# Transposing the residual in one visit per part, at other places in TensorE's order

## The chip, the cores and the metric

The kernel runs on one core of one Trainium2 chip. The metric is the device time of one execution in microseconds (us); smaller is better. Three executions of the kernel before took 1199.17, 1199.78 and 1201.17 us; their median, 1199.78 us, is the number that the change is compared with.

## The reference, cut to what matters

One decoder layer for 256 tokens of width 2048, in float32. The two places of the change are the two RMS norms behind a residual sum:

```python
x = x + mix @ w_out[i]                                   # w_out: 2048 x 2048

h2 = rms_norm(x, mlp_norm[i])
x = x + jnp.square(jax.nn.relu(h2 @ w_ffn_up[i])) @ w_ffn_down[i]   # 2048 x 8192, 8192 x 2048

gate = jax.nn.sigmoid(rms_norm(x, ple_norm[i]) @ w_ple_gate[i])
x = x + gate * (p[i] @ w_ple_proj[i])
...
return rms_norm(x, final_norm)
```

## The kernel before, in words

Every float32 operand is split into a high part and a rest (`wh` and `wl` for a weight, `h` and `l` for an activation), and a product is made of three float32r matmuls. A weight is loaded in blocks of 512 KB (`raw`, three buffers, by SyncE's DMA queue); ScalarE (ACT) copies it to `wh` in two halves (L149), VectorE (DVE) subtracts to get `wl` (L150). `wh` and `wl` have three buffers each as well, so the split of a block waits until TensorE (PE) is through with the block three places ahead of it. These splits have a raised priority in the scheduler.

The residual `xr` holds the tokens on the partitions, two tiles `x0` and `x1` of 128 tokens each. A product with `xr` as its input needs it the other way round. `transposed(name)` gives for that a function `part(norm, n)`, n from 0 to 3: it turns 512 columns of the residual, with 8 transposes of 128x128 on PE (L1018) into a pair of PSUM banks (`h2t` or `h3t`, the tag "wide" of the pool `psw`, which has two such pairs), and brings them to SBUF in four chunks of 128 columns, each with one ACT copy that scales by the norm's weight (L1024, the high part) and one DVE operation (L1025, the rest). Both read the same pair of banks, and the chunks of a pair follow each other: an ACT copy waits for the DVE operation of the chunk before it.

The stages around the change are these.

- **w_out**: four products `o0` to `o3` of 512 columns each, 48 matmuls of 512 columns each (four blocks of 12); behind each, `residual` adds it to `xr` on DVE (L956). Part n of `h2` follows `o`n in the code.
- **FFN up**: `gemm_wide` for 16 tiles, in two halves each of four blocks (`u00_0` to `u00_3` are the four blocks of the first half of tile 0). Block kq needs the chunks k = 4kq to 4kq+3 of `h2`, that is part kq. A chunk takes 4 matmuls, two of 512 columns (L997) and two of 256 (L1001).
- **FFN down**: `down_sweep` for two halves of the hidden units and two halves of the columns; the last sweep (names `d11`) writes the columns 1024 to 2047. Its four accumulators in the wide banks are released by DVE adds (L1131) after the step of kp 11, four steps before the last, and its other four banks at its end. `keep` splits blocks of the gate's weight ahead of time (`gk`, from `graw`).
- **p @ w_ple_proj**: four short products `pp0` to `pp3`, one block and 12 matmuls each, with ACT copies of the results out of PSUM (L1230). They use the bank pool `psm`. Three of the four square sums of the gate's norm (`junk`, L258) run there too, on ACT.
- **gate**: products `gt0` to `gt3`, which need all of `h3`.

PE's order up to the end of `w_out`'s first half is written by hand (`tc.manual_schedule` for PE, held open in `order`). From there on the scheduler orders all engines by priority; it may put the transposes anywhere between the matmuls once their inputs are expected to be ready. Parts 0 and 1 of `h3` read the columns 0 to 1023, which an earlier sweep finished; they are called from within the last sweep, by `between`, and parts 2 and 3 right behind it.

Of the kernel before, what the change touches and what calls it, by code (L numbers as in the profile page):

```python
# [40 lines left out]
def trunk(  # L41
# [931 lines left out]
    for g_ in o_a:  # L973
        finish(g_)
    order.close()
    rctx.close()
# [5 lines left out]

    def gemm_wide(src, acts, name, consume):

        for half in range(2):
            bank = wide_bank(f"{name}_w{half}")
            for kq in range(4):
                raw = load_raw(src[half, kq].rearrange("p a n -> p (a n)"), 1024, f"{name}{half}_{kq}")  # L990
                for a, (wh, wl) in enumerate(split_w(raw, f"{name}{half}_{kq}")):
                    for b in range(2):
                        k = kq * 4 + 2 * a + b
                        hl = acts(k)
                        for ct in range(2):
                            c = slice(b * 256 + ct * 128, b * 256 + ct * 128 + 128)
                            nc.tensor.matmul(  # L997
                                bank[:, ct, :].rearrange("p (s t) -> p s t", s=2), wh[:, c], hl,
                                start=k == 0, stop=False, skip_group_check=True,
                            )  # L1000
                            nc.tensor.matmul(  # L1001
                                bank[:, ct, 0:T], wl[:, c], hl[:, 0, :], start=False, stop=k == 15, skip_group_check=True
                            )
            consume(half, bank)

    def transposed(name):
# [3 lines left out]

        def part(norm, n):
            for j2 in range(2 * n, 2 * n + 2):
                if j2 % 2 == 0:
                    b = wide_bank(f"{name}t")
                for jj in range(2):
                    j = 2 * j2 + jj
                    for tt in range(2):
                        nc.tensor.transpose(  # L1018
                            b[:, j2 % 2, jj * T + tt * 128 : jj * T + (tt + 1) * 128], xr[tt][:, j * 128 : (j + 1) * 128], ident
                        )  # L1020
                for jj in range(2):
                    j = 2 * j2 + jj
# [9 lines left out]
    for n in range(4):  # L1032
        run(gemm_toks(w_out[n], mix, f"o{n}", lambda banks: residual(banks, n), (6, 7, 2, 3)))
        h2_part("mlp_norm", n)

# [52 lines left out]

    def down_sweep(hf, pair, ys, sboxes, hooks=(), between=None, seven=SEVEN):

# [42 lines left out]
        for q, kp in enumerate((0, 2, 1, 4, 3, *range(5, 16)) if pair else range(16)):  # L1133
# [32 lines left out]
            if kp == seven[-1]:  # L1166
# [9 lines left out]
                add(1, 1, b5)  # L1176
                if between is not None:
                    between()
        for n, tt, c in (("2", 0, 0), ("4", 1, 0), ("3", 0, 1), ("x", 1, 1)):
# [3 lines left out]
    def ffn_half(hf):  # L1183
        sboxes = {}
        ys = []
        for i in range(8):
# [12 lines left out]

            gemm_wide(w_up[f], h2, f"u{f}", square)  # L1200
            ys.append(y)
# [3 lines left out]
        if hf == 1:  # L1205
            h3_part, h3 = transposed("h3")
            h3_box.append(h3)

        down_sweep(hf, 0, ys, sboxes)
        if hf == 0:  # L1210
            down_sweep(hf, 1, ys, sboxes)
        else:
            down_sweep(hf, 1, ys, sboxes, {5: keep, 8: keep, 11: keep, 14: keep}, lambda: [h3_part("ple_norm", n) for n in range(2)], (1, 3, 6, 11))
            for n in range(2, 4):
                h3_part("ple_norm", n)

    ffn_half(0)
    ffn_half(1)
    h3 = h3_box[0]

# [5 lines left out]
    for n in range(4):  # L1226
# [4 lines left out]

        run(gemm_toks(w_proj[n], lambda k: (ph[:, k * T : (k + 1) * T], pl[:, k * T : (k + 1) * T]), f"pp{n}", copy_out))
    fn = a8(0, "fn")
    nc.sync.dma_start(fn, fnorm.partition_broadcast(128))
# [131 lines left out]
```

## Time and profile before

| | |
|---|---|
| median of three runs (lowest, highest) | 1199.78 us (1199.17, 1201.17) |
| the profiled execution, its own time | 1201.35 us |
| its span, first to last instruction | 1199.6 us |
| PE busy, share of the span | 1179.5 us, 98% |
| DVE busy | 868.5 us, 72% |
| ACT busy | 689.8 us, 58% |
| mean granted TensorE clock | 0.997 |

The durations below come from the profiled execution, which has 1.75 us around its span and took 1.57 us more than the median. In the timelines, the first column is the start in us from the span's beginning and the second the duration of the row's instructions together; "x8" is a row of eight instructions. A matmul's row lasts longer than the distance to the next one, since matmuls overlap: costs on PE are taken as differences of starts.

### The profile page before, as it was taken

The numbers are of one execution on the slowest core, as the hardware profiler recorded it, in microseconds if no ns is written. First come the engines' busy times: TensorE is split into PE (matmuls) and PEld (weight loads), VectorE is DVE, ScalarE is ACT, GpSimd is POOL, SyncE is SP. The second block draws the span as 40 slices with busy tenths as digits, with TensorE's granted clock in tenths as the row PEclk, the third lists the DMA queues.
The fourth block names the chain that finished last, engine by engine and source line by source line (L and its number), as shares of the span: only waits on it lengthen the run. The fifth ranks groups of instructions, "written<-read, shape, count | busy, mean of one in ns | idle before, by whom it ended". The sixth has DMA issues, their size and how long they took to land.

```text
span 1199.6 us, 18428 instructions
## 1 busy us (share of the span) xinstructions
PE 1179.5 (98%) x7060; PEld 1010.6 (84%) x7060; DVE 868.5 (72%) x1149; ACT 689.8 (58%) x1276; POOL 18.1 (2%) x69
## 2 busy tenths in 40 slices
PE   8999999999999999999999999999999999999997
PEld 6999988987887888888888788888888888777886
DVE  7687987965656666666878888666667879787552
ACT  6857566566545565555655564454555555668544
POOL 4000010000000000000000000000000000000000
PEclk9999999999999999999999999999999999999999
DMA  6463542354445555555665656655555556766531
GB/s 246 154 201 109 175 144 104 113 198 141 140 163 179 184 185 190 192 191 189 201 201 200 193 195 211 191 181 188 189 184 189 207 194 197 287 231 211 195 120 70
DMA packets 60328, 216.88 MB, mean 181 GB/s; under 512 B 6736, under 2 KB 7120, under 8 KB 59856
## 3 DMA queue, kind: packets, MB, share of 16 engines
q1 hardware_dynamic: 59952, 215.19, 53.4%
q8 instruction: 55, 0.90, 0.3%
q10 hardware_dynamic: 288, 0.52, 0.1%
q14 instruction: 33, 0.27, 0.1%
HBM read 213.59 MB, written 2.10 MB: 180 GB/s over the span
## 4 chain that ended last, share of the span: by engine, by line
PE 81%; DVE 8%; DMA 4%; ACT 4%; issue 2%; SPq 0%; ACTq 0%; DVEq 0%
PE u_w L997 20%; PE u_w L1001 10%; PE d_b L1112 5%; PE d_b L1113 5%; PE d_b L1111 5%; DMA raw_d<-in_w_ffn_down_dram 3%; PE gt_b L171 2%; PE gt_b L173 2%; PE gt_b L172 2%; PE wag_b L331 1%; PE zp_b L171 1%; PE o_b L171 1%; PE o_b L172 1%; PE o_b L173 1%; PE d_w L1112 1%
## 5 line engine op out<-in xcount | busy, mean ns | idle before, releaser
L997 PE MATMUL u_w<-h,wh_u 128*128 128x512 f32 x1024 | 358.8, 395 | 0.0
L1001 PE MATMUL u_w<-h,wl_u 128*128 128x256 f32 x1024 | 287.3, 281 | 0.0
L149 ACT ACTIVATE wh_u<-raw_u 128x512 fp32r<-128x512 f32 x256 | 147.6, 624 | 166.2 <-PE u_w L997 93.1
L150 DVE TENSOR_TENSOR wl_u<-raw_u,wh_u 128x1024 fp32r<-128x1024 f32 x128 | 156.7, 1225 | 115.1 <-ACT wh_u L149 115.1
L997 PEld LDWEIGHTS u_w<-h,wh_u 128*128 128x128 f32 x1024 | 192.0, 187 | 44.8
L1001 PEld LDWEIGHTS u_w<-h,wl_u 128*128 128x128 f32 x1024 | 193.6, 189 | 0.0
L150 DVE TENSOR_TENSOR wl_gt<-raw_gt,wh_gt 128x1024 fp32r<-128x1024 f32 x24 | 29.4, 1225 | 23.9 <-ACT wh_gt L149 23.9
L149 ACT ACTIVATE wh_gt<-raw_gt 128x512 fp32r<-128x512 f32 x48 | 27.8, 631 | 23.0 <-PE gt_b L173 18.8
L1151 DVE TENSOR_TENSOR td<-raw_d 128x512 f32<-128x512 f32 x22 | 15.2, 693 | 31.0 <-DMA raw_d<-in_w_ffn_down_dram 31.0
L162 PE MATMUL zv_b<-hTh,wh_zv 128*128 128x256 f32 x128 | 37.6, 294 | 0.0
L171 PE MATMUL gt_b<-wh_gt,h 128*128 128x512 f32 x96 | 37.5, 390 | 0.0
L162 PE MATMUL zr_b<-hTh,wh_zr 128*128 128x256 f32 x128 | 37.4, 292 | 0.0
L173 PE MATMUL gt_b<-wh_gt,h 128*128 128x512 f32 x96 | 37.4, 389 | 0.0
L172 PE MATMUL gt_b<-wl_gt,h 128*128 128x512 f32 x96 | 37.4, 389 | 0.0
L164 PE MATMUL zr_b<-hTh,wl_zr 128*128 128x256 f32 x128 | 37.0, 289 | 0.1
L163 PE MATMUL zr_b<-hTl,wh_zr 128*128 128x256 f32 x128 | 37.0, 289 | 0.0
L162 PE MATMUL zk_b<-hTh,wh_zk 128*128 128x256 f32 x128 | 36.9, 288 | 0.0
L163 PE MATMUL zk_b<-hTl,wh_zk 128*128 128x256 f32 x128 | 36.3, 284 | 0.5 <-DVE hTl L155 0.5
L164 PE MATMUL zk_b<-hTh,wl_zk 128*128 128x256 f32 x128 | 36.3, 284 | 0.1
L163 PE MATMUL zv_b<-hTl,wh_zv 128*128 128x256 f32 x128 | 36.2, 283 | 0.0
L164 PE MATMUL zv_b<-hTh,wl_zv 128*128 128x256 f32 x128 | 36.2, 283 | 0.0
L154 ACT ACTIVATE wad<-raw_d 128x512 fp32r<-128x512 f32 x22 | 13.9, 632 | 33.7 <-DMA raw_d<-in_w_ffn_down_dram 29.1
(807 smaller groups left out, 3077.6 us busy)
## 6 DMA issues: line engine op xcount, KB each, us to landing
raw_u<-in_w_ffn_up_dram SPq DMA_DIRECT2D x128, 512.0 KB, 3.6
raw_d<-in_w_ffn_down_dram SPq DMA_DIRECT2D x128, 512.0 KB, 4.0
raw_gt<-in_w_ple_gate_dram SPq DMA_DIRECT2D x24, 512.0 KB, 3.5
raw_zk<-in_w_in_dram SPq DMA_DIRECT2D x16, 512.0 KB, 3.3
raw_zr<-in_w_in_dram SPq DMA_DIRECT2D x16, 512.0 KB, 3.4
raw_zv<-in_w_in_dram SPq DMA_DIRECT2D x16, 512.0 KB, 3.2
raw_zp<-in_w_in_dram SPq DMA_DIRECT2D x16, 512.0 KB, 3.3
raw_o<-in_w_out_dram SPq DMA_DIRECT2D x16, 512.0 KB, 3.5
```

The source lines that it names most:

```text
L149: nc.scalar.activation(wh[:, a * 512 : (a + 1) * 512], raw[:, a * 512 : (a + 1) * 512], AF.Copy)
L150: nc.vector.tensor_tensor(wl, raw, wh.bitcast(F32), op=ALU.subtract)
L162: nc.tensor.matmul(o, w_h, ah, start=first and ct % 2 == 0, stop=False, skip_group_check=True)
L163: nc.tensor.matmul(o, w_h, al, start=False, stop=False, skip_group_check=True)
L164: nc.tensor.matmul(o, w_l, ah, start=False, stop=last, skip_group_check=True)
L171: nc.tensor.matmul(o, a_h, wh[:, 0:n], start=first, stop=False)
L172: nc.tensor.matmul(o, a_h, wl[:, 0:n], start=False, stop=False)
L173: nc.tensor.matmul(o, a_l, wh[:, 0:n], start=False, stop=last)
L997: nc.tensor.matmul(bank[:, ct, :].rearrange("p (s t) -> p s t", s=2), wh[:, c], hl, start=k == 0, stop=False, skip_group_check=True,)
L1001: nc.tensor.matmul(bank[:, ct, 0:T], wl[:, c], hl[:, 0, :], start=False, stop=k == 15, skip_group_check=True)
L1111: nc.tensor.matmul(banks[n], ah, wh, start=first, stop=False)
L1112: nc.tensor.matmul(banks[n], ah, wl, start=False, stop=False)
```

## The change

PE's order by hand is now held open until block `u0` of FFN up has been written, and opened again for PE from the last sweep of FFN down to the end of the `pp` products. In such a stretch PE's instructions stand in the order of the code; the other engines are still ordered by the scheduler. `part` now issues its 8 transposes before its evacuations, and in a pair of banks of its own each time. The calls are moved:

```diff
-    order.close()
     rctx.close()
...
-    def gemm_wide(src, acts, name, consume):
+    def gemm_wide(src, acts, name, consume, hooks=()):
...
             for kq in range(4):
+                if (half, kq) in hooks:
+                    hooks[half, kq]()
                 raw = load_raw(src[half, kq].rearrange("p a n -> p (a n)"), 1024, f"{name}{half}_{kq}")
...
         def part(norm, n):
+            b = wide_bank(f"{name}t")
             for j2 in range(2 * n, 2 * n + 2):
-                if j2 % 2 == 0:
-                    b = wide_bank(f"{name}t")
                 for jj in range(2):
...
+            for j2 in range(2 * n, 2 * n + 2):
                 for jj in range(2):
                     j = 2 * j2 + jj
                     src = b[:, j2 % 2, jj * T : (jj + 1) * T]
...
         run(gemm_toks(w_out[n], mix, f"o{n}", lambda banks: residual(banks, n), (6, 7, 2, 3)))
-        h2_part("mlp_norm", n)
+        if n:
+            h2_part("mlp_norm", n - 1)
...
-            gemm_wide(w_up[f], h2, f"u{f}", square)
+            gemm_wide(w_up[f], h2, f"u{f}", square, {} if f else {(0, 3): lambda: h2_part("mlp_norm", 3)})
+            if f == 0:
+                order.close()
...
-            down_sweep(hf, 1, ys, sboxes, {5: keep, 8: keep, 11: keep, 14: keep}, lambda: [h3_part("ple_norm", n) for n in range(2)], (1, 3, 6, 11))
-            for n in range(2, 4):
+            order.enter_context(tc.manual_schedule(engines={mybir.EngineType.PE}))
+            down_sweep(hf, 1, ys, sboxes, {5: keep, 8: keep, 11: keep, 14: keep}, (1, 3, 6, 11))
+            for n in range(2):
                 h3_part("ple_norm", n)
...
         run(gemm_toks(w_proj[n], lambda k: (ph[:, k * T : (k + 1) * T], pl[:, k * T : (k + 1) * T]), f"pp{n}", copy_out))
+        if n == 1:
+            for i in range(2, 4):
+                h3_part("ple_norm", i)
+    order.close()
```

The numbers of instructions are the same on PE. In the program before, each part of `h2` is transposed in three visits of 1, 3 and 4 transposes, part 3 within `u00_0` and `u00_1`; parts 0 and 1 of `h3` take visits of 4, 8 and 4 within the last four steps of the sweep, and parts 2 and 3 visits of 4, 1, 3 and 8 around `pp0` and in `pp2`. Now parts 0 to 2 of `h2` stand behind `o1`, `o2` and `o3` and part 3 between `u00_2` and `u00_3`; parts 0 and 1 of `h3` stand together behind the sweep's last matmul, and parts 2 and 3 together between `pp1` and `pp2`.

PE before, from the last matmul of `o3` (`mp1` is the mixer's output, `h2t_4195` the banks of part 3):

```order
L173 MATMUL o3_b1_4116<-wh_o3_3_4176,mp1_3688 128x512
L1018 MATMUL h2t_4195<-ident_78,x0_3157 128x128
L997 MATMUL u0_w0_4214<-h2_3823,wh_u00_0_4217 128x512
L1001 MATMUL u0_w0_4214<-h2_3823,wl_u00_0_4218 128x256
L997 MATMUL u0_w0_4214<-h2_3823,wh_u00_0_4217 128x512
L1018 MATMUL h2t_4195<-ident_78,x1_3158 128x128
```

PE now, the last two of part 3's eight transposes (`h2t_4266`) and what follows them:

```order
L1018 MATMUL h2t_4266<-ident_78,x0_3157 128x128
L1018 MATMUL h2t_4266<-ident_78,x1_3158 128x128
L998 MATMUL u0_w0_4196<-h2_3822,wh_u00_3_4285 128x512
L1002 MATMUL u0_w0_4196<-h2_3822,wl_u00_3_4286 128x256
L998 MATMUL u0_w0_4196<-h2_3822,wh_u00_3_4285 128x512
```

The transposes of part 3 moved from the first blocks of `u00` to the place right ahead of the block that reads them.

ACT before, at the beginning of FFN up (all evacuations here are of part 3):

```order
L149 ACTIVATE wh_u00_2_4263<-raw_u00_2_4261 128x512 x2
L1024 ACTIVATE h2_3823<-h2t_4195,par_sb_70 128x256 x2
L149 ACTIVATE wh_u00_3_4286<-raw_u00_3_4284 128x512 x2
L1024 ACTIVATE h2_3823<-h2t_4195,par_sb_70 128x256 x2
L149 ACTIVATE wh_u01_0_4316<-raw_u01_0_4314 128x512 x2
L149 ACTIVATE wh_u01_1_4339<-raw_u01_1_4337 128x512 x2
```

ACT now, at the same place (`h2t_4177` is part 2, `h2t_4266` part 3):

```order
L1025 ACTIVATE h2_3822<-h2t_4177,par_sb_70 128x256 x2
L149 ACTIVATE wh_u00_3_4285<-raw_u00_3_4283 128x512 x2
L1025 ACTIVATE h2_3822<-h2t_4177,par_sb_70 128x256
L149 ACTIVATE wh_u01_0_4315<-raw_u01_0_4313 128x512 x2
L1025 ACTIVATE h2_3822<-h2t_4177,par_sb_70 128x256
L149 ACTIVATE wh_u01_1_4338<-raw_u01_1_4336 128x512 x2
L1025 ACTIVATE h2_3822<-h2t_4266,par_sb_70 128x256 x4
L149 ACTIVATE wh_u01_2_4361<-raw_u01_2_4359 128x512 x2
```

Part 2's last chunk now stands behind the split of `u01_0`, and all of part 3 behind that of `u01_1`; the DVE halves stand in the same way behind the `wl` of those blocks.

ACT before, during the `pp` products (`h3t_10291` is part 2, `h3t_10308` part 3):

```order
L149 ACTIVATE wh_pp3_0_10406<-raw_pp3_0_10404 128x512 x2
L1024 ACTIVATE h3_8876<-h3t_10291,par_sb_70 128x256
L1024 ACTIVATE h3_8876<-h3t_10308,par_sb_70 128x256
L1230 ACTIVATE pp0_10331<-pp0_b0_10333 128x512
L1230 ACTIVATE pp1_10332<-pp0_b1_10334 128x512
L149 ACTIVATE wh_gt0_0_10446<-raw_gt0_0_10444 128x512 x2
L1024 ACTIVATE h3_8876<-h3t_10291,par_sb_70 128x256
```

ACT now, at the same place (`h3t_10259` is part 0, `h3t_10276` part 1, `gk7` half a split of the gate's weight):

```order
L1059 ACTIVATE gk7_10709<-graw7_10707 128x512
L1025 ACTIVATE h3_8876<-h3t_10259,par_sb_70 128x256
L149 ACTIVATE wh_pp3_0_10408<-raw_pp3_0_10406 128x512 x2
L1025 ACTIVATE h3_8876<-h3t_10259,par_sb_70 128x256
L1025 ACTIVATE h3_8876<-h3t_10276,par_sb_70 128x256
L1233 ACTIVATE pp0_10299<-pp0_b0_10301 128x512
L1233 ACTIVATE pp1_10300<-pp0_b1_10302 128x512
L149 ACTIVATE wh_gt0_0_10449<-raw_gt0_0_10447 128x512 x2
L1025 ACTIVATE h3_8876<-h3t_10259,par_sb_70 128x256
L1025 ACTIVATE h3_8876<-h3t_10276,par_sb_70 128x256
```

The evacuations of parts 0 and 1 moved from the sweep into this stretch, and part 0's fourth and last one stands behind the split of `gt0`'s first block. On DVE the order is the same: `wl_gt0_0`, then part 0's last chunk.

More of the change, by code (lines that the diff above doesn't have):

```diff
@@ L1087, in activation_sums, with down_sweep @@
         split_sb(st[:, 0:512], st[:, 512:1024], t_[:, 0:512])
-    def down_sweep(hf, pair, ys, sboxes, hooks=(), between=None, seven=SEVEN):
+    def down_sweep(hf, pair, ys, sboxes, hooks=(), seven=SEVEN):
         nm = f"d{hf}{pair}"
@@ L1176, in down_sweep @@
                 add(1, 1, b5)
-                if between is not None:
-                    between()
         for n, tt, c in (("2", 0, 0), ("4", 1, 0), ("3", 0, 1), ("x", 1, 1)):
@@ L1206, in ffn_half @@
             h3_part, h3 = transposed("h3")
-            h3_box.append(h3)
+            h3_box.extend((h3_part, h3))
         down_sweep(hf, 0, ys, sboxes)
@@ L1218, in trunk @@
     ffn_half(1)
-    h3 = h3_box[0]
+    h3_part, h3 = h3_box
     praw = load_raw(pT.rearrange("p a t -> p (a t)"), 512, "pT")
```

## The prediction

> **What bounds the kernel now.** I read the page first, then TensorE's (PE's) timeline around the two places, then those of ScalarE (ACT) and VectorE (DVE) there. The page's busy times, and its chain of work that ended last by engine:
>
> ```profile
> PE 1179.5 (98%) x7060; PEld 1010.6 (84%) x7060; DVE 868.5 (72%) x1149; ACT 689.8 (58%) x1276; POOL 18.1 (2%) x69
> PE 81%; DVE 8%; DMA 4%; ACT 4%; issue 2%; SPq 0%; ACTq 0%; DVEq 0%
> ```
>
> PE is the bound: each microsecond that it stands still, or spends on a transpose, is in the time. So I price PE at both places, by starts. First `w_out` and the beginning of FFN up: the first matmuls of `o0`, `o1`, `o2`, `o3`, the first transpose of part 3, the first matmul of `u00`, of block `u00_1`, of `u01` and of the next tile:
>
> ```profile
> 341.01 0.39 PE L171 MATMUL o_b<-wh_o,mg 128*128 128x512 f32 x1
> 351.89 0.39 PE L171 MATMUL o_b<-wh_o,mg 128*128 128x512 f32 x1
> 363.91 0.39 PE L171 MATMUL o_b<-wh_o,mg 128*128 128x512 f32 x1
> 375.99 0.39 PE L171 MATMUL o_b<-wh_o,mg 128*128 128x512 f32 x1
> 388.64 0.33 PE L1018 MATMUL h2t<-ident,x 128*128 128x128 f32 x1 [0.43 <-DVE x L956]
> 388.74 0.47 PE L997 MATMUL u_w<-h,wh_u 128*128 128x512 f32 x1
> 391.96 0.40 PE L997 MATMUL u_w<-h,wh_u 128*128 128x512 f32 x1
> 400.73 0.39 PE L997 MATMUL u_w<-h,wh_u 128*128 128x512 f32 x1
> 411.83 0.39 PE L997 MATMUL u_w<-h,wh_u 128*128 128x512 f32 x1
> ```
>
> `o0` has no transposes: 351.89 - 341.01 = 10.88 us for 48 matmuls, 0.227 each. `o1`, `o2`, `o3` take 12.02, 12.08 and 12.75, and the first half of `u0` 11.99 against 11.10 of the second (0.69 for each of 16 chunks). The transposes of `h2` with their waits cost 1.14 + 1.20 + 1.87 + 0.89 = 5.10 us.
>
> The end of the last sweep: three matmuls around a visit of eight transposes, then around one of four:
>
> ```profile
> 1071.95 0.39 PE L1113 MATMUL d_b<-wh_d_13b,y 128*128 128x512 f32 x1
> 1073.30 1.09 PE L1018 MATMUL h3t<-ident,x 128*128 128x128 f32 x8 [0.96 <-DVE x L1131]
> 1074.47 0.40 PE L1112 MATMUL d_b<-wl_d_13b,y 128*128 128x512 f32 x1
> 1079.95 0.39 PE L1112 MATMUL d_b<-wl_d_14b,y 128*128 128x512 f32 x1
> 1080.53 0.66 PE L1018 MATMUL h3t<-ident,x 128*128 128x128 f32 x4 [0.20 <-DVE h L1025]
> 1081.26 0.39 PE L1111 MATMUL d_b<-wh_d_14b,y 128*128 128x512 f32 x1
> ```
>
> Two matmuls lie between the outer starts of each three, 0.45 us. So the eight cost 2.52 - 0.45 = 2.07 with their wait, the four 1.31 - 0.45 = 0.86. Last, the `pp` products: the sweep's last matmul, the end of `pp1`, the start of `pp2`, its visit of eight, and the first of `gt0`:
>
> ```profile
> 1087.87 0.39 PE L1113 MATMUL d_b<-wh_d_15b,y 128*128 128x512 f32 x1
> 1094.91 0.39 PE L173 MATMUL pp_b<-wh_pp,pl 128*128 128x512 f32 x1
> 1096.15 0.50 PE L171 MATMUL pp_b<-wh_pp,ph 128*128 128x512 f32 x1 [0.84 <-ACT pp L1230]
> 1096.48 0.40 PE L172 MATMUL pp_b<-wl_pp,ph 128*128 128x512 f32 x1
> 1096.72 1.04 PE L1018 MATMUL h3t<-ident,x 128*128 128x128 f32 x8
> 1097.82 0.40 PE L171 MATMUL pp_b<-wh_pp,ph 128*128 128x512 f32 x1
> 1102.67 0.50 PE L171 MATMUL gt_b<-wh_gt,h 128*128 128x512 f32 x1
> ```
>
> A visit of eight without a wait costs 1097.82 - 1096.48 - 0.45 = 0.89 us. From the sweep's last matmul to `gt0` it takes 14.80 us, and one of its waits is for ACT: that engine is the one to look at there.
>
> **The change, first place.** Four visits of eight are 4 x 0.89 = 3.56 us instead of 5.10: 1.54 less if nothing waits. The wait for the residual at 388.64 goes, since part n is now transposed one product later. What is late next are the evacuations. Parts 0 and 1 have `o2` and `o3` to be brought out under, more than 10 us each, and cost nothing. Part 3 stands right ahead of its reader, and in ACT's queue its chunks stand behind the split of `u01_1`, which needs the buffer of `u00_2`: it cannot start before PE is through with `u00_2`, the moment at which the transposes start. Such a step of before, on ACT and then DVE (`wl` of that block ran on DVE just ahead of the chunk at 394.42):
>
> ```profile
> 392.09 1.15 ACT L149 ACTIVATE wh_u<-raw_u 128x512 fp32r<-128x512 f32 x2 [0.49 <-PE u_w L997]
> 390.62 0.48 DVE L1025 SCALAR_TENSOR_TENSOR h<-h2t,par_sb,h 128x256 fp32r<-128x256 f32 x1
> 391.64 0.48 DVE L1025 SCALAR_TENSOR_TENSOR h<-h2t,par_sb,h 128x256 fp32r<-128x256 f32 x1 [0.54 <-ACT h L1024]
> 394.42 0.48 DVE L1025 SCALAR_TENSOR_TENSOR h<-h2t,par_sb,h 128x256 fp32r<-128x256 f32 x1
> ```
>
> The block's end (391.96) released the split at 392.09; DVE reached a chunk at 394.42 and was done 0.48 later, 2.94 us behind the block's end. So `u00_3` waits 2.94 - 0.89 = 2.05 us behind its transposes. Its other three chunks come every 391.64 - 390.62 = 1.02 us (each ACT copy waits for the DVE operation before it) and are used in 0.69: 3 x 0.33 = 0.99 more. Part 2's last chunk stands behind the split of `u01_0`, released when `u00_2` starts; it is needed 3 x 0.69 = 2.07 later and there after 2.94: 0.87. Sum: 3.56 + 2.05 + 0.99 + 0.87 - 5.10 = **+2.4 us**. Bounds: if no split stood ahead, one chunk of 1.02 + the 0.99 less the visit would leave 3.56 + 1.12 - 5.10 = -0.4; with one more split of 2.33 (394.42 - 392.09) ahead, +4.7. I take the middle, which the order shows.
>
> **Second place.** The sweep loses its visits and their waits: 2.07 + 0.86, and half of 0.89 for the other visit of four, 3.38 us. ACT and DVE lose eight evacuations there. Behind the sweep's last matmul PE now has two visits, 1.78, and `pp0` and `pp1`, 24 x 0.227 = 5.44; with the last matmul itself it is at part 2's transposes after 7.45 us. The pairs of banks are two, so these wait until part 0 has been brought out, all of it: its last chunk stands behind `wh` and `wl` of `gt0`'s first block. The same chain of before, ACT from the split of `pp1` on, then DVE:
>
> ```profile
> 1088.64 2.40 ACT L149 ACTIVATE wh_pp<-raw_pp 128x512 fp32r<-128x512 f32 x4 [3.05 <-DMA raw_pp<-in_w_ple_proj_dram]
> 1091.31 1.05 ACT L258 ACTIVATE junk_n<-x 128x1024 f32<-128x1024 f32 x1
> 1092.35 0.46 ACT L1024 ACTIVATE h<-h3t,par_sb 128x256 fp32r<-128x256 f32 x1
> 1093.74 1.14 ACT L149 ACTIVATE wh_pp<-raw_pp 128x512 fp32r<-128x512 f32 x2
> 1094.79 0.82 ACT L1024 ACTIVATE h<-h3t,par_sb 128x256 fp32r<-128x256 f32 x2
> 1095.50 1.09 ACT L1230 ACTIVATE pp<-pp_b 128x512 f32<-128x512 f32 x2
> 1096.45 1.17 ACT L149 ACTIVATE wh_gt<-raw_gt 128x512 fp32r<-128x512 f32 x2
> 1097.65 1.23 DVE L150 TENSOR_TENSOR wl_gt<-raw_gt,wh_gt 128x1024 fp32r<-128x1024 f32 x1 [0.72 <-ACT wh_gt L149]
> 1098.79 0.87 DVE L1025 SCALAR_TENSOR_TENSOR h<-h3t,par_sb,h 128x256 fp32r<-128x256 f32 x2
> ```
>
> From 1088.64 ACT has no gap: it is the bound of this stretch already. To DVE's chunk behind `wl_gt` it is 1098.79 + 0.48 - 1088.64 = 10.63 us. The new order has the same work and one chunk more (0.71 / 2 = 0.36, the pair at 1094.79) and half a gate split more (1.05 / 2 = 0.52): 11.5. The chain began 0.77 us behind the sweep's last matmul, when a DMA landed; now PE reaches that matmul up to 3.38 us earlier, while the loads follow splits that gain less. The shift lies between 0 and +3.4; I take +1.0, so the banks come free 1.8 + 11.5 = 13.3 us behind the last matmul, and PE waits 13.3 - 7.45 = 5.85. For part 3's transposes part 1's last chunk must go: on ACT two chunks, two copies of results, a square sum of 1.04 (1092.35 - 1091.31) later. That is 1.92 us behind part 0's, less the visit of 0.89: 1.03 more. `pp2` starts at 13.3 + 1.92 + 0.89 = 16.1, `gt0` after 24 matmuls at 21.55, against 14.80. In `gt0` the splits are in time again. Sum: 21.55 - 14.80 - 3.38 = **+3.4 us**, from +2.4 to +5.8. The old wait of `pp2` (0.84) is inside the 14.80.
>
> **The clock.** Before shows what little work on PE does to it, in three windows (PE's time and count, then the granted clock, third from the end):
>
> ```profile
> 146.78:150.19 3.41, 2.74 (x20) 2.28 (x20) 3.41 (x5) 0.57 (x2) 0.00 (x0) 1.00 0.46 154
> 150.20:153.61 3.41, 3.41 (x19) 3.41 (x18) 3.41 (x7) 2.62 (x6) 0.00 (x0) 0.50 0.50 154
> 153.61:157.02 3.41, 3.41 (x30) 3.41 (x30) 3.39 (x4) 1.15 (x2) 1.10 (x2) 1.00 0.42 154
> ```
>
> Behind a window with 20 matmuls the clock was 0.50 for 3.41 us, and 19 ran instead of 30: 11 / 30 x 3.41 = 1.25 us lost. From 7.45 to 16.1 PE has nothing but 16 transposes, more than two such windows; a drop in there reaches into `pp2`. I take +1.3, between 0 (over before `pp2`) and 2.6 (two windows). In FFN up the empty stretch is about 3 us; there I take 0, with 1.3 as the other end. [...]
>
> **Sum.** 2.4 + 3.4 + 1.3 = +7.1 us: 1206.9 from the median of 1199.78. The profiled execution, 1201.35 with 1.75 around its span, would be 1208.5.
>
> **Rivals.** *No clock loss.* Both waits, but the drop is over when `pp2` starts: +5.8, 1205.6. For it speaks that a drop here lasted one window only. [...]
>
> *The loads are later still.* ACT's queue now has half a gate split, with its own load, ahead of the split of the sweep's last block, so PE can wait there too and the chain starts at the upper end: 2.4 more, 1209.3.
>
> *FFN up hides its wait*, if the evacuations slip ahead: -0.4 instead of +2.4, so 1204.1. The queues are in order; against it.
>
> *Waits half as long.* 1.95 off the first sum, 3.4 off the second and no clock loss leave about +0.4: 1200.2.
>
> *The visits pay: faster.* If part 0 were out before PE reaches part 2, in 7.45 us instead of 13.3, and FFN up did not wait, the gains would stand alone: 1.54 + 3.38, and 14.80 - (0.23 + 3.56 + 48 x 0.227) = 0.1, together 5.0: 1194.8. It is decided at part 0's last chunk; only if the split of `gt0`'s first block, which needs `pp1` finished, stood behind it.
>
> That the change does not do what it says is excluded by the order: the visits stand where the code puts them.
>
> **Numbers.** Forecast 0.51, no clock loss 0.24, later loads 0.12, FFN up hidden 0.05, half waits 0.04, faster 0.04. A measurement of this kernel tells about 0.2%, 2.4 us, from no change: faster 0.04, same 0.04, slower 0.92. The range goes from no clock loss with the loads as before, 1206.9 - 1.3 - 1.0 = 1204.6, to later loads and a drop in FFN up as well, 1206.9 + 2.4 + 1.3 = 1210.6.
>
> **What would show it.** PE's timeline: a wait of about 2 us in front of `u00_3` that DVE's chunk ends, one near 0.9 within `u00_2`; in front of part 2's `h3t` a wait of 5 to 6 us ended by DVE L1026, and about 1 before part 3's; no waits in the sweep's last steps; a record of clock 0.50 that reaches into `pp2`. I am wrong if PE finds the banks free at part 2, or if the sweep's end does not come some 3 us sooner relative to its start.

## The result, and the profile after

Ten executions of the changed kernel took 1209.07 us in the median (1203.21 to 1215.65), ten of the kernel before on the same chip 1201.58 (1198.65 to 1204.36). The ratio is 1.0072, with a 95% interval of 1.0056 to 1.0088: slower by 8.7 us (6.7 to 10.6) by the ratio, by 7.5 by the medians. The forecast was 1206.9, from 1204.6 to 1210.6, or +7.1.

The profiled execution took 1208.12 us, its span is 1206.4. The page's busy times and its chain of work that ended last, by engine:

```profile
PE 1179.9 (98%) x7060; PEld 1013.6 (84%) x7060; DVE 868.6 (72%) x1149; ACT 689.9 (57%) x1276; POOL 17.6 (1%) x69
PE 53%; DMA 6%; DVE 4%; ACT 3%; issue 2%; SPq 0%; ACTq 0%; DVEq 0%
```

PE is as busy as before, 1179.9 us against 1179.5, in a span that is 6.8 us longer. Nearly all of the added time is PE standing still, and it stands at the two places. The chain's shares add up to only 68% here, so the account goes by PE's timeline. First that from `o0` to the tile behind `u0`, with the visit of part 3 (the chunks' matmuls are now L998, the evacuations L1025 on ACT and L1026 on DVE):

```profile
339.56 0.39 PE L171 MATMUL o_b<-wh_o,mg 128*128 128x512 f32 x1
...
385.69 0.48 PE L998 MATMUL u_w<-h,wh_u 128*128 128x512 f32 x1
...
393.29 0.28 PE L1002 MATMUL u_w<-h,wl_u 128*128 128x256 f32 x1
394.32 0.50 PE L998 MATMUL u_w<-h,wh_u 128*128 128x512 f32 x1 [0.75 <-DVE h L1026]
...
395.13 1.03 PE L1018 MATMUL h2t<-ident,x 128*128 128x128 f32 x8
...
398.11 0.50 PE L998 MATMUL u_w<-h,wh_u 128*128 128x512 f32 x1 [1.95 <-DVE h L1026]
...
399.14 0.50 PE L998 MATMUL u_w<-h,wh_u 128*128 128x512 f32 x1
...
413.09 0.39 PE L998 MATMUL u_w<-h,wh_u 128*128 128x512 f32 x1
```

From `o0` to the tile behind `u0` it takes 413.09 - 339.56 = 73.53 us, against 70.82 before: +2.71. Two waits are new, 0.75 us within `u00_2` and 1.95 behind part 3's transposes, both ended by DVE's chunk. Behind the second one the chunks come 399.14 - 398.11 = 1.03 us apart. What ACT and DVE did there, ahead of the chunk that PE waited for:

```profile
395.25 1.15 ACT L149 ACTIVATE wh_u<-raw_u 128x512 fp32r<-128x512 f32 x2 [2.28 <-issue]
396.31 0.46 ACT L1025 ACTIVATE h<-h2t,par_sb 128x256 fp32r<-128x256 f32 x1
396.44 1.23 DVE L150 TENSOR_TENSOR wl_u<-raw_u,wh_u 128x1024 fp32r<-128x1024 f32 x1 [2.17 <-ACT wh_u L149]
397.58 0.48 DVE L1026 SCALAR_TENSOR_TENSOR h<-h2t,par_sb,h 128x256 fp32r<-128x256 f32 x1
```

The split started when PE had left `u00_2` (395.25), and the chunk behind it was there at 397.58 + 0.48 = 398.06, 2.81 us later. Second place, PE from the sweep's step `d_12a` to `gt0`:

```profile
1063.70 0.39 PE L1113 MATMUL d_b<-wh_d_12a,y 128*128 128x512 f32 x1
...
1075.15 0.50 PE L1114 MATMUL d_b<-wl_d_14a,y 128*128 128x512 f32 x1 [0.19 <-DVE wl_d_14a L1125]
...
1084.29 0.50 PE L1114 MATMUL d_b<-wl_d_15b,y 128*128 128x512 f32 x1 [0.43 <-DVE wl_d_15b L1125]
...
1086.71 0.39 PE L1115 MATMUL d_b<-wh_d_15b,y 128*128 128x512 f32 x1
1086.94 1.91 PE L1018 MATMUL h3t<-ident,x 128*128 128x128 f32 x16
1089.05 0.47 PE L171 MATMUL pp_b<-wh_pp,ph 128*128 128x512 f32 x1 [0.20 <-DVE x L1133]
...
1094.44 0.39 PE L173 MATMUL pp_b<-wh_pp,pl 128*128 128x512 f32 x1
1100.08 3.91 PE L1018 MATMUL h3t<-ident,x 128*128 128x128 f32 x16 [5.25 <-DVE h L1026]
1103.64 0.78 PE L171 MATMUL pp_b<-wh_pp,ph 128*128 128x512 f32 x1
...
1109.60 0.39 PE L171 MATMUL gt_b<-wh_gt,h 128*128 128x512 f32 x1
```

Before, the first matmul of the same step was this:

```profile
1062.85 0.39 PE L1111 MATMUL d_b<-wh_d_12a,y 128*128 128x512 f32 x1
```

The sweep's last steps are 2.0 us shorter (1086.71 - 1063.70 = 23.01, before 1087.87 - 1062.85 = 25.02), with two small waits for splits; from the last matmul to `gt0` it is 22.89 us against 14.80. In between stands the wait of 5.25 us for DVE's chunk of part 0. The queues of ACT and DVE read thus, from ACT's splits for `pp1` and `pp2` on:

```profile
1087.72 1.15 ACT L149 ACTIVATE wh_pp<-raw_pp 128x512 fp32r<-128x512 f32 x2 [1.49 <-DMA raw_pp<-in_w_ple_proj_dram]
1089.66 1.15 ACT L149 ACTIVATE wh_pp<-raw_pp 128x512 fp32r<-128x512 f32 x2 [0.78 <-DVE x L1133]
...
1097.10 1.18 ACT L149 ACTIVATE wh_gt<-raw_gt 128x512 fp32r<-128x512 f32 x2
1098.14 0.87 ACT L1025 ACTIVATE h<-h3t,par_sb 128x256 fp32r<-128x256 f32 x2
1098.31 1.23 DVE L150 TENSOR_TENSOR wl_gt<-raw_gt,wh_gt 128x1024 fp32r<-128x1024 f32 x1 [0.73 <-ACT wh_gt L149]
1099.45 0.87 DVE L1026 SCALAR_TENSOR_TENSOR h<-h3t,par_sb,h 128x256 fp32r<-128x256 f32 x2
```

The first of the last two DVE operations is part 0's last chunk; its end, 1099.45 + 0.48 = 1099.93, is what PE's transposes at 1100.08 waited for. Three windows of this stretch (PE's time and count come first behind the window's length, the granted clock is third from the end), and PE's weight loads of part 3's transposes:

```profile
1094.32:1097.74 3.42, 0.51 (x3) 0.08 (x1) 2.49 (x4) 3.42 (x9) 0.00 (x0) 1.00 0.60 240
1097.74:1101.15 3.41, 1.07 (x5) 1.11 (x6) 2.12 (x4) 3.41 (x9) 0.00 (x0) 0.50 0.58 174
1101.15:1104.56 3.41, 3.38 (x15) 2.89 (x14) 2.40 (x6) 2.25 (x6) 0.00 (x0) 0.50 0.35 138
```

```profile
1102.02 1.57 PEld L1018 LDWEIGHTS h3t<-ident,x 128*128 128x128 f32 x8 [0.41 <-PE h3t L1018]
```

Behind the nearly empty window (0.51 us of PE's time) the clock was 0.50 for two windows. A visit of eight took some 1.6 us in it instead of 0.89.

The two places make +2.71 and +6.08 (45.90 us from `d_12a` to `gt0`, 39.82 before), 8.8 in all. The two profiled executions differ by 6.8, since the one of after reached `o0` 1.45 us sooner and was 0.4 us shorter between the places.

### The profile page after: what moved, and what is told of

It is laid out like the page before. It is cut to its first block, busy times and chain, and to the rows that moved or that the text cites. A ratio compares the mean times of both kernels' runs of the same rounds, so it can differ in the third digit from the quotient of the medians.

```text
span 1206.4 us, 18426 instructions
## 1 busy us (share of the span) xinstructions
PE 1179.9 (98%) x7060; PEld 1013.6 (84%) x7060; DVE 868.6 (72%) x1149; ACT 689.9 (57%) x1276; POOL 17.6 (1%) x69
## 4 chain that ended last, share of the span: by engine, by line
PE 53%; DMA 6%; DVE 4%; ACT 3%; issue 2%; SPq 0%; ACTq 0%; DVEq 0%
PE u_w L998 19%; PE u_w L1002 10%; DMA raw_d<-in_w_ffn_down_dram 5%; PE d_b L1114 4%; PE d_b L1113 4%; PE d_b L1115 4%; PE gt_b L172 2%; PE gt_b L171 2%; PE gt_b L173 2%; PE d_w L1114 1%; PE d_w L1115 1%; PE d_w L1113 1%; DMA graw<-in_w_ple_gate_dram 1%; DVE td L1154 1%; PE h3t L1018 0%
## 5 line engine op out<-in xcount | busy, mean ns | idle before, releaser
L998 PE MATMUL u_w<-h,wh_u 128*128 128x512 f32 x1024 | 359.3, 395 | 2.9 <-DVE h L1026 2.7
L998 PEld LDWEIGHTS u_w<-h,wh_u 128*128 128x128 f32 x1024 | 192.0, 187 | 49.0 <-DVE h L1026 4.4
```

Of the source, the lines that this page charges most:

```text
L998: nc.tensor.matmul(bank[:, ct, :].rearrange("p (s t) -> p s t", s=2), wh[:, c], hl, start=k == 0, stop=False, skip_group_check=True,)
```

## The experiments

All are compared with the kernel before on the same chip, mostly 12 executions each. A total resolves only some 2 us here (the last section says why), so each run is also read by its profile: "first" is PE's time from the first matmul of `o0` to the tile behind `u0`, "second" from the sweep's step `d_12a` to `gt0`, both by starts in PE's timeline. A profile is one execution, and not always a typical one: those of e2, e7 and e10 took 1210.88, 1190.63 and 1197.23 us where the medians are 1205.07, 1197.86 and 1203.36.

| run | time, from before (95%), us | first | second | 0.50 behind the place |
|---|---|---|---|---|
| before | 0 | 70.81 | 39.82 | no |
| after | +8.7 (6.7, 10.6) | 73.53 | 45.90 | second |
| e1_first_only | +2.4 (0.8, 4.0) | 74.43 | 37.37 | first |
| e2_second_only | +4.0 (1.7, 6.1) | 71.29 | 46.49 | second |
| e3_behind_pp3 | +2.5 (0.6, 4.4) | 73.53 | 39.94 | second |
| e4_chunks_first | +2.4 (1.0, 3.8) | 73.29 | 39.93 | first |
| e5_part3_two_blocks_up | +4.7 (2.4, 7.1) | 74.99 | 38.63 | first |
| e6_one_block_up | -1.3 (-3.4, 0.6) | 70.36 | 38.46 | no |
| e7_both_places_mended | -2.8 (-4.8, -0.7) | 69.34 | 37.33 | no |
| e8_changed_again | one run, 1212.40 us | 73.74 | 45.04 | second |
| e9_other_banks | -3.8 (-6.0, -1.6) | 69.29 | 38.28 | no |
| e10_mended_without_priority | +2.4 (0.2, 4.7) | 70.36 | 39.48 | no |
| e11_issue_order_only | +1.4 (-0.4, 3.1) | 70.88 | 38.71 | no |
| e12_mended_other_banks | -1.7 (-3.5, 0.0) | 69.34 | 37.87 | no |

**One place at a time.** The first experiment takes the second place back to the scheduler, the second one the first place.

```diff
# e1_first_only, against the changed kernel
-            order.enter_context(tc.manual_schedule(engines={mybir.EngineType.PE}))
-            down_sweep(hf, 1, ys, sboxes, {5: keep, 8: keep, 11: keep, 14: keep}, (1, 3, 6, 11))
-            for n in range(2):
+            down_sweep(hf, 1, ys, sboxes, {5: keep, ...}, lambda: [h3_part("ple_norm", n) for n in range(2)], (1, 3, 6, 11))
+            for n in range(2, 4):
                 h3_part("ple_norm", n)
...
-        if n == 1:
-            for i in range(2, 4):
-                h3_part("ple_norm", i)
-    order.close()
# e2_second_only, against the changed kernel
+    order.close()
     rctx.close()
...
-        if n:
-            h2_part("mlp_norm", n - 1)
+        h2_part("mlp_norm", n)
...
-            gemm_wide(w_up[f], h2, f"u{f}", square, {} if f else {(0, 3): lambda: h2_part("mlp_norm", 3)})
-            if f == 0:
-                order.close()
+            gemm_wide(w_up[f], h2, f"u{f}", square)
```

Both keep the third piece of the change, the new issue order in `part`.

> Only the first place is changed: parts 0 to 2 of h2 behind o1, o2 and o3, part 3 between u00_2 and u00_3, TensorE's order by hand to the end of u0; the last sweep and the pp products are ordered by the scheduler as before. Theory (the loss has two causes that add up): in the changed kernel's trace it takes 413.09 - 339.56 = 73.53 us from the first matmul of o0 to the tile behind u0, against 411.83 - 341.01 = 70.82 before, so +2.7 us, with waits of 0.75 us within u00_2 and 1.95 us before u00_3, no clock record of 0.50 in FFN up and none in the pp products. Rival (all of the loss is made in the pp products, and what u00 waits is made up later in FFN up, whose splits run ahead of TensorE again): 0 us, within 1.0.

> Only the second place is changed: w_out and FFN up as before, parts 0 and 1 of h3 behind the sweep's last matmul, parts 2 and 3 between pp1 and pp2. Theory: from the sweep's step d_12a to its last matmul 2.0 us less than before, from there to gt0 8.1 us more (22.9 against 14.8), a wait of about 5.4 us before part 2's transposes and a clock record of 0.50 that begins in it: +6.1 us. With the first experiment's +2.7 that is 8.8, a little above what the changed kernel lost. Rival (the wait for the banks comes from loads that are late because the first place was late too): then the wait is much shorter here, under 3 us, the clock stays at 1.00 and the loss is under +3.5 us.

Both places cost: +2.4 us for the first, +4.0 (at most 6.1) for the second, 6.4 together against 8.7 (6.7 to 10.6) for both. In the profiles it is +3.62 us in the first stage of e1 and +6.67 in the second of e2, where 6.1 was expected. e1's second stage is 2.45 us shorter than before, so its total is less than its first stage; for e2 the total is also less than the stage, in a profile that took 5.8 us more than the median. In e2 the wait before part 2 was there without the first place, and no shorter, so its rival fell:

```profile
1103.01 3.91 PE L1019 MATMUL h3t<-ident,x 128*128 128x128 f32 x16 [6.32 <-DVE h L1027]
```

In one point the expectation of e1 was wrong: it had no clock record in FFN up. The window that holds the wait of 1.95 us, and the one behind it, in e1, then the corresponding window of the changed kernel, whose waits were the same to 0.01 us:

```profile
397.04:400.45 3.41, 1.46 (x11) 1.17 (x10) 1.72 (x3) 1.95 (x4) 0.00 (x0) 1.00 0.48 149
400.45:403.87 3.42, 3.42 (x12) 2.68 (x11) 1.35 (x3) 0.95 (x2) 0.00 (x0) 0.50 0.40 146
```

```profile
394.59:398.00 3.41, 1.57 (x12) 1.25 (x11) 1.56 (x2) 1.51 (x3) 0.00 (x0) 1.00 0.56 154
```

In e1 the window holds the whole wait, and PE's time in it is 1.46 us; in the changed kernel the window ends before the wait does, and 1.57 us are left. Of e1's 74.43 us, 73.53 are those of the changed kernel, 0.7 the clock and 0.2 a slower pace of the matmuls (last section).

**Something else in the gap.** Parts 2 and 3 of `h3` behind `pp3`, so that `pp2` and `pp3` lie where PE waited.

```diff
-        if n == 1:
+        if n == 3:
             for i in range(2, 4):
                 h3_part("ple_norm", i)
```

> The changed kernel, with parts 2 and 3 of h3 transposed behind pp3 instead of between pp1 and pp2. Theory (PE stands still because the banks are late and nothing else is placed there): pp2 and pp3, 24 matmuls or 5.4 us, lie where it waited 5.4 us. They need the banks of pp0 and pp1, whose copies were through at 1097.2 and 1099.9, so about 2.5 us of wait stay before pp2, too short for a clock record of 0.50; gt0 begins some 5 us earlier than in the changed kernel, and the kernel is at +2.0 to +3.0 us from before. Rival (ACT's backlog is what counts, and it only moves: gt0 waits for the evacuations of parts 2 and 3, which now come later): gt0's blocks 2 and 3 wait for DVE's chunks, and the kernel stays at +5 us or more.

The gap was filled: 39.94 us instead of 45.90, and +2.5 us, which is what the first place costs alone. As expected, a wait for a copy of `pp0` stayed, 1.91 us long; that it would be too short for the clock was an estimate, and wrong:

```profile
1097.65 0.50 PE L171 MATMUL pp_b<-wh_pp,ph 128*128 128x512 f32 x1 [1.91 <-ACT pp L1233]
```

```profile
1095.31:1098.73 3.42, 1.51 (x7) 0.92 (x7) 2.50 (x4) 3.42 (x9) 0.00 (x0) 1.00 0.27 107
1098.73:1102.14 3.41, 3.41 (x10) 2.63 (x9) 2.01 (x3) 2.10 (x5) 0.00 (x0) 0.50 0.61 172
```

The next window ran at 0.50 and held 8 matmuls some 0.43 us apart instead of 0.227: 1.6 us.

**The queue's order.** The evacuations get a higher priority than the splits of weights.

```diff
-                    nc.scalar.activation(h[:, j, :], src, AF.Copy, scale=col(norm, j))
-                    nc.vector.scalar_tensor_tensor(...)
+                    with tc.high_priority(25000):
+                        nc.scalar.activation(h[:, j, :], src, AF.Copy, scale=col(norm, j))
+                        nc.vector.scalar_tensor_tensor(...)
```

> The changed kernel with one thing more: the evacuations' ACT copies and DVE operations have a higher priority than the splits of weights, so that in the queues of ACT and DVE the last chunk of part 2 of h2 stands ahead of the split of u01_0, and the last chunk of part 0 of h3 ahead of the copies of pp0 and the split of gt0's first block. Part 3 of h2 still stands behind the split of u01_1. Theory (the chunks are late because splits and copies stand ahead of them): the 0.75 us within u00_2 goes, the 1.95 before u00_3 stays; before part 2 of h3 the wait falls from 5.4 by 2 to 3 us, which leaves no clock record of 0.50 behind it (1.2 us): +2.0 to +4.0 us from before instead of +7.5. Rival (the chunks' own pace on ACT and DVE, 1.02 us each one behind the other, sets the wait, whatever stands between them): no more than 1 us is gained, +6.5 to +7.5.

The wait within `u00_2` is gone, the one before `u00_3` is 1.95 as before, and before part 2 and part 3 of `h3` PE waits 2.38 and 0.56 us:

```profile
1094.70 1.06 PE L1018 MATMUL h3t<-ident,x 128*128 128x128 f32 x8 [2.38 <-DVE h L1027]
...
1096.33 1.06 PE L1018 MATMUL h3t<-ident,x 128*128 128x128 f32 x8 [0.56 <-DVE h L1027]
```

What stood ahead of the chunks was worth 2.9 us of the 5.25; what is left is ACT's other work in that stretch and the chunks' own pace. There is no record of 0.50 at the second place, but this time one behind `u00_3`, and +2.4 us.

**Further up.** Part 3 of `h2` between `u00_0` and `u00_1` (e5); with parts 0 to 2 one block into the next product as well (e6); and e5 with part 3 in two single banks that `w_out` has left (e9). All three leave the second place to the scheduler.

```diff
# e5, against e1
-            gemm_wide(..., {} if f else {(0, 3): lambda: h2_part("mlp_norm", 3)})
+            gemm_wide(..., {} if f else {(0, 1): lambda: h2_part("mlp_norm", 3)})
# e6, also
-        run(gemm_toks(w_out[n], mix, f"o{n}", lambda banks: residual(banks, n), (6, 7, 2, 3)))
-        if n:
-            h2_part("mlp_norm", n - 1)
+        hooks = {7: lambda: h2_part("mlp_norm", n - 1)} if n else {}
+        run(gemm_toks(w_out[n], mix, f"o{n}", lambda banks: residual(banks, n), (6, 7, 2, 3), hooks))
# e9, against e5
-            b = wide_bank(f"{name}t")
+            if norm == "mlp_norm" and n == 3:
+                b = [mm_bank(f"{name}t{i}") for i in range(2)]
+            else:
+                wide = wide_bank(f"{name}t")
+                b = wide[:, 0], wide[:, 1]
```

> The first experiment (first place only) with part 3 of h2 transposed between u00_0 and u00_1 instead of between u00_2 and u00_3. Theory (a place further up doesn't help, since of the two pairs of banks u0's accumulator has one and part 2 the other): PE waits 3 to 5 us before part 3's transposes until DVE is through with part 2's last chunk; the waits within u00_2 and before u00_3 go, so the stage costs what it cost in the first experiment: +1.5 to +3.5 us from before. Rival (the place alone was wrong): no wait at either point, the four visits cost 3.56 us instead of 5.10, -1.5 us.

> As the run before, with parts 0, 1 and 2 of h2 also one block further up: each is transposed one block (2.72 us) into the next product instead of... behind it, that is part n behind the first block of o(n+1). Theory: part 2 then leaves its pair of banks before PE reaches part 3's place, part 3 has two blocks (5.5 us) in which to be brought out, and the four visits cost 3.56 us with at most 1 us of wait: -1.5 to -0.5 us from before, no clock record of 0.50 in FFN up. Rival (a chunk leaves only once per split wherever the visit stands, 2.7 us each): four chunks take some 11 us, PE waits 3 us or more at u00_3, +1.5 us or more.

> The fifth experiment (first place only, part 3 of h2 between u00_0 and u00_1), with part 3 in two single banks of the pool that the products of w_out have left (tag mm) instead of a pair of the wide pool; its two banks are evacuated as two tiles. Theory (the 3.94 us before part 3 were the pair of banks, held by part 2): no wait before part 3's transposes; its chunks are out within the two blocks (5.5 us) ahead of u00_3; the stage from o0 to the tile behind u0 falls from 70.82 us before to 69.3 to 70.3, so the kernel is at -1.5 to -0.5 us from before. Rival (the wait was for the residual sum or for ACT, and the banks only came free at the same time): PE still waits 3 us or more there, +1.5 to +4 us as in the fifth experiment.

The place alone did not mend it: `u0`'s accumulator has one of the two pairs, part 2 the other, and the two waits became one before part 3's transposes, in e5:

```profile
393.52 1.08 PE L1018 MATMUL h2t<-ident,x 128*128 128x128 f32 x8 [3.94 <-DVE h L1026]
```

A window with 0.91 us of PE's time lies in it, and the one behind it ran at 0.50, so the first stage (74.99 us) and the time (+4.7) are above what was expected. With part 2 out sooner (e6) the only wait left is one of 0.75 us at `u00_3`, 70.36 us. The total of e6, -1.3, is within its noise (-3.4 to 0.6). In other banks (e9) nothing waits, at the same place in PE's order as in e5: 69.29 us, 1.52 less than before, the four visits without waits. So the 3.94 were the pair. How ACT and DVE worked off these chunks in e9:

```profile
390.94 1.19 ACT L1029 ACTIVATE h<-h2t,par_sb 128x256 fp32r<-128x256 f32 x3
392.21 2.05 DVE L1030 SCALAR_TENSOR_TENSOR h<-h2t,par_sb,h 128x256 fp32r<-128x256 f32 x5
```

By the order of the program the three copies read part 2's pair and each of part 3's single banks; they follow each other without a gap. Chunks of one pair had a pitch of 1.02 us. The time of e9, -3.8 us, is more than its first stage explains and than was expected. Its second stage is 1.54 us shorter as well, but e11 below has most of that without a gain in time; where the rest comes from is open.

**Both places by hand, mended.** Parts 0 to 2 of `h2` as in e6, part 3 between `u00_0` and `u00_1`, the parts of `h3` ahead of the sweep's steps 13 and 15 and behind `pp0` and `pp2`, evacuations first as in e4.

```diff
-            down_sweep(hf, 1, ys, sboxes, {5: keep, 8: keep, 11: keep, 14: keep}, (1, 3, 6, 11))
-            for n in range(2):
-                h3_part("ple_norm", n)
+            down_sweep(hf, 1, ys, sboxes, {5: [keep], 8: [keep], 11: [keep], 13: [lambda: h3_part("ple_norm", 0)], 14: [keep], 15: [lambda: h3_part("ple_norm", 1)]}, (1, 3, 6, 11))
...
-        if n == 1:
-            for i in range(2, 4):
-                h3_part("ple_norm", i)
+        for i in {0: (2,), 2: (3,)}.get(n, ()):
+            h3_part("ple_norm", i)
```

> Both places by hand, mended: parts 0 to 2 of h2 one block into the next product and part 3 between u00_0 and u00_1; part 0 of h3 ahead of the sweep's step 13, part 1 ahead of step 15, part 2 behind pp0, part 3 behind pp2; the evacuations ahead of the splits in priority. Theory: first place 3.56 us instead of 5.10, -1.5; from d_12a to gt0 the matmuls alone are 21.5 + 0.2 + 48 x 0.227 = 32.6 us and four visits 3.56, together 36.2, with at most 1 us of wait for the banks at part 0 and 1 for splits, against 39.8 before: -1.6 to -3.6. In all -3 to -5 us, no clock record of 0.50 at either place. Rival (chunks ahead of splits only move the wait to the weights' splits, in w_out, in the sweep and before gt0): within 1 us of before.

> The seventh experiment (both places mended) without the priority of the evacuations ahead of the splits; the places of the transposes are the same. Theory (places and queue order both count: a chunk behind a split and two copies leaves its pair late): at the first place 0.5 to 1 us is lost (u00_3 waits 0.75, as in the sixth experiment), at the second PE waits 2 to 3 us before the transposes of part 3, behind pp2, for the pair of part 1 or 2: d_12a to gt0 39 to 41 us instead of 37.3, and the kernel is within 1.5 us of before. Rival (the places alone made the gain): 37 to 38 us there, and -2 to -4 us from before again.

> The seventh experiment (both places by hand and mended, evacuations ahead of splits) with part 3 of h2 in the two single banks of the ninth. Theory (the two gains add up): 69.3 us from o0 to the tile behind u0 (-1.5), 37.3 from d_12a to gt0 (-2.5), -3.0 to -5.0 us from before. Rival (the second place by hand is worth nothing beyond what the issue order in part gives): -3.8 us or less gain, no better than the ninth experiment.

e7 is faster than before, by 2.8 us (0.7 to 4.8), just under the 3 to 5 expected: the first stage is 1.47 us shorter, the second 2.49, and the only wait from the sweep's step 12 to `gt0` that the timeline shows is

```profile
1079.32 0.47 PE L171 MATMUL pp_b<-wh_pp,ph 128*128 128x512 f32 x1 [0.84 <-DVE x L1133]
```

Without the priority (e10) the same places lose 1.02 us in the first stage and 2.15 in the second, most of it in one wait before part 3 of `h3`:

```profile
1095.05 1.06 PE L1018 MATMUL h3t<-ident,x 128*128 128x128 f32 x8 [2.31 <-DVE h L1026]
```

That is what was expected of the stages; the total, +2.4 (0.2 to 4.7), is above the 1.5 and above what the stages give. The profiled execution was among the fastest of its kernel, 6.1 us under the median, so it doesn't show what the others lost; that is open. e12 is about as short in the stages as e7 (whose first place had no wait left that other banks could take away), and by time, -1.7 (-3.5 to 0.0), it is less than the 3 to 5 expected and not better than e7 or e9: the three intervals overlap.

**What the issue order in `part` does alone** (8 transposes, then the evacuations, nothing else changed).

> Only the third piece of the change: part issues its 8 transposes before its evacuations; places, pools and the scheduler are as before. Theory (the scheduler then puts the eight transposes into two visits instead of three and mends the second place by itself, as the stretch from d_12a to gt0 shows in the four experiments that left the second place to it: 37.36, 38.63, 38.46 and 38.28 us against 39.82): that stretch 37.3 to 38.7 us, the stage from o0 to the tile behind u0 70.3 to 70.9, and -1.2 to -3.0 us from before. Rival (those shorter stretches came from the first place's other timing): 39.8 us there, 0 within 1 us.

The second stage was 38.71 us in its profile, at the upper end of what was expected, the first 70.88; the time, +1.4 (-0.4 to 3.1), shows no gain, and the expected -1.2 to -3.0 lie outside its interval. What the shorter stage is worth stays inconclusive: 39.82 is one profile of before, and a stage that ends on loads moves by about 1 us from run to run (45.90 and 45.04 for the same code).

**The changed kernel again.**

> The changed kernel once more, for one profile. Theory (the clock is granted in windows of 3.41 us whose grid has no fixed phase against the program; a window with under about 0.4 of PE's work is followed by one at 0.50): the wait of over 5 us before part 2 always holds such a window, so a record of 0.50 stands in the pp products again; the waits of FFN up (0.75 and 1.95 us and a visit between) hold one only for some phases, so a record of 0.50 near u00_3 may be there this time, though the code is the same and the first profile had none. Rival (the record in FFN up belongs to the kernel, not to the phase): none in FFN up, as in the first profile.

The wait before part 2 was 6.17 us and again two windows at 0.50 followed. In FFN up there was none:

```profile
395.02:398.43 3.41, 1.62 (x12) 1.29 (x11) 1.52 (x2) 1.51 (x3) 0.00 (x0) 1.00 0.49 154
```

So this run does not tell the phase from the kernel. The bound of the theory, about 0.4 of a window, was an estimate: before it, in these two stages, the windows with 0.51 us of PE's time (after), 1.46 (e1), 1.47 (e4) and 1.51 (e3), 0.15 to 0.44 of 3.41 us, had been followed by one at 0.50, and one with 1.57 us, 0.46, had not (after); here 0.39 us was and 1.62 was not. e1, e3 and e4 tell the two apart for FFN up: with the same wait of 1.95 us, e1 and e4 had a record of 0.50, e3 and the two profiles of the changed kernel had none, and PE's order at this place is the same in all of them.

## Why the prediction was right, point by point

- **First place**, forecast +2.4, measured +2.71. The visits without waits, e9 shows, do give the 1.5 us that the sum had. The idle times in the rows, 1.95 and 0.75, begin at the modelled end of the matmul before. Counted by starts, as the forecast counts, the wait of 2.05 us behind part 3's transposes was 398.11 - 395.13 - 0.89 = 2.09, and the 0.87 within `u00_2` was 394.32 - 393.29 - 0.12 = 0.91 (0.12 is the usual distance behind a matmul of 256 columns). The chunks' pitch was 1.03 (forecast 1.02). The 0.3 that the sum lacked are mostly the first matmuls behind these waits, each some 0.1 us slower. e4 takes away the splits ahead of part 2 and with them the wait within `u00_2` alone.
- **The sweep's visits**, forecast -3.38, measured -2.0 in the changed kernel, -2.3 in e2, -3.5 in e3, e4 and e8. This term was mis-sized for some runs: with the visits gone, splits of the last steps are just in time or just late. The forecast named it as a sign of being wrong if the sweep's end did not come some 3 us sooner; in this profile it came 2.0 sooner, and behind two waits that it had ruled out.
- **The banks at part 2**, forecast free 13.3 us behind the sweep's last matmul; part 2's transposes started 1100.08 - 1086.71 = 13.37 us behind it, in e2 and e8 14.5 and 14.3. That the sum is met so closely is luck: the forecast's ACT chain was to begin 1.8 us behind that matmul and to take 11.5; it began 1087.72 - 1086.71 = 1.01 behind it and took 1099.93 - 1087.72 = 12.21, with a gap of 0.78 in it. PE was at part 2 after 7.96 us instead of 7.45, since `pp0` began 0.33 later, waiting for the residual, and `pp0` and `pp1` took 5.62 instead of 5.44. So by starts it waited 13.37 - 7.96 = 5.41 for a forecast 5.85. e3 and e4 show that it was both: an order with nothing else to do, and a queue in which the last chunk stood behind a split.
- **Part 3**, to begin 1.92 us behind part 2 (the forecast gives no working for this figure), began 1102.02 - 1100.08 = 1.94 behind it. Of that 0.41 was wait, for a forecast 1.03: the visit of part 2 ran at half clock and covered the rest.
- **The clock**, forecast +1.3. Part 3's visit began at 1102.02, when DVE was through with part 1; its last chunk took DVE 0.48 us in this window at 0.50, as a chunk of before did at 1.00. At full clock part 3's visit would have been over 0.89 later, at 1102.91. It was over at 1103.64, and `pp2` and `pp3` took 5.96 us instead of 5.44. That is 0.73 + 0.52 = 1.25 us. The forecast had the size from the matmuls that one window lost before; here more than half of it is a visit at half clock, so the agreement to 0.05 us is partly luck. The rival without a clock loss fell. In FFN up, where 0 was taken, it is 0 or 0.7 from run to run.
- **The rivals.** Later loads: e2 and e8 go 1 us that way, not 2.4; there ACT waited 1.91 and 1.63 us for the weights of `pp2`. A hidden wait in FFN up and half waits did not come; ACT and DVE worked in the program's order there, the split at 395.25 and the chunk behind it at 396.31, and on DVE 396.44 and 397.58. The visits that pay are real, but not with this order: e7 has them with the banks free in time.

Taken from the trace, the terms make +8.8 where the forecast had +7.1. The 1.7 are the sweep's 1.4 and 0.3 of the first place.

## What to carry to other kernels

A transpose by hand ends when its banks have been read, not when PE has left it: look where the evacuation stands in the queues of the two engines that do it, and give it more distance than the splits ahead of it take (in the changed kernel PE waited 5.25 us for a chunk behind a split). Two pairs of banks that transposes share with an accumulator are one pair: 3.94 us of wait in e5, none in other banks in e9. An empty stretch on PE cost more by the clock in two runs, 0.7 us behind 1.95 us in e1 and 1.6 behind 1.91 in e3, and nothing behind 1.95 in the changed kernel. Here it gained the same to fill the gap of the second place with matmuls that were ready (e3) and to shorten it (e4): 39.94 and 39.93 us.

## What the runs showed of the hardware that was not expected

**Windows with 1.5 us of PE's work were followed by one at clock 0.50, and the windows' grid did not follow the program.** In the stages of the two places a window of 3.41 us with 0.00 to 1.51 us of PE's time was followed by one at 0.50 (1.46 in e1, 1.51 in e3), one with 1.57 or more was not (1.57 in after, 1.62 in e8). At about 150 us into the program, among smaller instructions, one with 2.74 us was, as the prediction's row shows, and in the changed kernel one with 3.29 at 138.59, so this bound holds for these stages only. The records in a profile lie whole windows apart, in the changed kernel's at 142.01 and 1097.74 us, 280 times 3.413. The wait of 1.95 us ended 0.11 us behind the end of its window there (398.11, 398.00) and 0.59 ahead of it in e1 (399.86, 400.45). So the same stretch of PE's order with the same wait of 1.95 us loses 0.7 us in one run and nothing in another.

**FFN up has two paces.** The first matmul of the second eight tiles and the first of the sweep behind them, in the changed kernel, then in e7:

```profile
736.02 0.39 PE L998 MATMUL u_w<-h,wh_u 128*128 128x512 f32 x1
...
916.91 0.40 PE L1113 MATMUL d_b<-wh_d_0a,y 128*128 128x512 f32 x1
```

```profile
730.85 0.39 PE L998 MATMUL u_w<-h,wh_u 128*128 128x512 f32 x1
...
908.38 0.39 PE L1113 MATMUL d_b<-wh_d_0a,y 128*128 128x512 f32 x1
```

The same 1024 matmuls took 180.89 and 177.53 us, without a wait in either: each of 16 halves 11.31 or 11.09. In the changed kernel, which has the faster pace in the first eight tiles and the slower one here, the difference is all in the matmuls of 512 columns: at the faster pace the next one starts 230 ns behind each, at the slower one some 233, 236 and 241 ns by turns, while behind those of 256 columns it is 117 ns on average at both. In the profiles of before and of the changed kernel a stage kept its pace, 11.09 us for every half behind the first in the first eight tiles and 11.29 to 11.31 for all 16 here. Of the 14 profiles, 12 had the slower one in this stage and 3 in the stage of the first eight tiles. It is worth 3.4 us here. The changed kernel's own two profiles had both in the first eight tiles (11.09 us a half, and 11.31 in e8), so the code alone does not set it; what does is open. It is one reason why the totals scatter by several us.

**The chunks of one pair follow each other, two banks or not.** On one pair an ACT copy waited for the DVE operation of the chunk before it, 1.02 to 1.03 us a chunk, also from the first of its banks to the second; on different tiles (e9) three copies took 1.19 us together. It is the program that keeps them apart, by semaphores and tile by tile; what the chip would do without them was not tried.
